# A hybrid encoder layer on one core: first weight units in two pieces, and value rows whose splits are placed later

## The chip, the core and the metric

The kernel runs on one core of a Trainium2 chip. A core has a matrix engine (TensorE, PE in the rows; PEld is its load of stationary weights), a vector engine (VectorE, DVE), a scalar engine (ScalarE, ACT), GpSimd (POOL) and SyncE (SP), which only starts transfers here. Each engine works through its own instructions in the order in which they were written, and waits for the others by semaphores. A transfer runs on up to 16 DMA engines. The metric is the device time of one execution in microseconds.

## The reference, cut to what matters

One encoder layer on a sequence of 512 tokens of width 1024, in float32.

```python
proj = h @ w_in[l]
qa, ka, va, qb, kb, vb = jnp.split(proj, SPLITS, axis=-1)
qa = rope_partial(qa.reshape(b, s, A_Q_HEADS, HEAD_DIM), pos)      # first quarter of each head is rotated
ka = rope_partial(ka.reshape(b, s, A_KV_HEADS, HEAD_DIM), pos)
...
o_a = windowed_gqa_sink(qa, ka, va, a_sink[l]).astype(h.dtype)     # 128-query blocks, window 128, a sink per head
o_b = dilated_mixture(qb, kb, vb).astype(h.dtype)                  # windows (128,1), (512,4), (2048,16)
gates = jax.nn.sigmoid(h @ w_gate[l] + b_gate[l])
g_a, g_b = jnp.split(gates, N_BRANCH, axis=-1)
mixed = g_a * (o_a @ w_br_a[l]) + g_b * (o_b @ w_br_b[l])
y = mixed @ w_out[l]
h = layer_norm(DN_ALPHA * h + y, ln1_g[l], ln1_b[l])
f = (jax.nn.silu(h @ w_ff_gate[l]) * (h @ w_ff_up[l])) @ w_ff_down[l]
h = layer_norm(DN_ALPHA * h + f, ln2_g[l], ln2_b[l])
```

## The kernel before, in words

**Products.** Every operand of a product is split into a high part, rounded to the format that TensorE takes, and the rest (`split`, L349: a copy on ScalarE or VectorE, then a subtraction on VectorE). A product of two operands is three matmuls of 128x512: high by high, high by low, low by high (L453 to L455 in `feat_k`; L626 to L628 for value rows). x stands turned, as eight tiles of 128x512 (`xT`), of which the first four belong to half 0 of a weight unit and the others to half 1. A weight unit has 128 output columns; a half unit is a transfer of 256 KB.

**The order.** No engine's order is written by hand. Each piece of work is an `op` with a cost for each engine that may do it, the tiles that it reads and writes, and a priority. `Program.run` (L170) plays the program through with these costs: at each moment every free engine takes the ready operation of lowest priority number for which buffers are there, and so the instructions are written down. A transfer on SyncE occupies two running counters (start of issue, end of data) and is taken to be done 0.9 us after its data. If a planned transfer is faster than the real one, the operations that need it stand too early in their engine's queue, and all behind them wait as well.

**The start** (`half_unit_by`, L366). The first three half units (a key unit k and two query units q and r of the first mixer) come in three pieces each of 128, 128 and 256 columns (`CUTS`). The table `FIRST` gives the priority of each piece and of each tile of x. PE takes x's tiles one after the other, with nine matmuls each (three units by three). Behind them come a third query unit (q2) and the values.

**Value rows** (`token_values`, L596). For the four residues of a token's place modulo 4 the value rows of both mixers are computed (a row is 24 matmuls: eight weights by three), evicted and written to a scratch tensor in DRAM (`aside`, L638; `va` in the rows). When all four are there, twelve transfers read them back: four for the left 256 columns in blocks of the first mixer (L644), eight of half the size for the right 256 columns in windows of the second (L650). `value_split` (L581) makes high and low parts of 128x256 of each of the eight results: a copy (L332 or L334) and a subtraction (L588).

**Rotation** (`Turn`, L471). The rows to be rotated are gathered into one tile (L482), rotated with cos and sin on VectorE (L493 to L499) and put back (L503). The tables for it, the masks, the sinks and the identity are loaded near the start (L432 to L437).

**Attention** (`unit_a`, L708). For a block of 128 queries and four heads: scores on PE (L575, L576), mask and minimum on VectorE (L724), exponential on ScalarE (L728), sum's reciprocal (L731), normalising (L664 on ScalarE, L666 on VectorE), transposes of the probabilities on PE (L676), their split, and the product with the values (L741, L742). The table `ORDER` lists the stages: `q2 VA T G A0 q3 ...` means query unit 2, value rows, rotation, a gate unit, the four blocks of head group 0 of the first mixer, query unit 3. The dense units (`q`, `k1`, `G`) are the work that PE has beside the attention.

Of the kernel before, what the change touches and what calls it, by code (L numbers as in the profile page):

```python
# [15 lines left out]
P = 128  # L16
S = 512
# [42 lines left out]

CUTS = ((0, 128), (128, 256), (256, 512))
FIRST = {("k", 0): (-1000, -998.2, -997.2), ("q", 0): (-998.8, -998.1, -997.1), ("r", 0): (-998.7, -998, -997),
         ("k", 1): (-996.9,), ("q", 1): (-996.7,), ("r", 1): (-996.6,),
         "x": (-999.9, -998.5, -997.5, -996.95, -996.8, -996.5, -996.4, -996.3)}
N_WS, N_WHL, N_ATT, N_WHL1, N_TWO = 6, 16, 16, 40, 4
# [8 lines left out]
ORDER = """  # L74
q2 VA T G A0 q3 q4 G k1 T A1 q5 G q6 q7 T A2 G G A3 Q00 K00 T V Q02 K02 T Q01 K01 T B0 B1 G g Q10 K10 T g Q12 K12 T Q11 K11 T B2 B3 g8
"""
# [20 lines left out]
class Program:  # L97
# [72 lines left out]
    def run(self):  # L170
# [28 lines left out]
        while n_left:  # L199
# [11 lines left out]
            while progress:  # L211
                progress = False
                for e in engines:
# [65 lines left out]
def dve(n, fast=False, extra=0.0):  # L279
    return 0.069 + (0.00074 if fast else 0.00104) * n + extra  # L280
# [7 lines left out]
def hybrid_layer(ctx: ExitStack, tc: tile.TileContext, wpack, xT, xtok, sink, bgate,  # L288
# [145 lines left out]
    load(mA, maska, abs_prio=-119.3, dst=lambda: mA.t[:, :384])  # L434
    load(nsink, sink.partition_broadcast(P), 0.1, abs_prio=-119.2)
    load(ident, identd, 0.2, abs_prio=-119.1)
    load(bg, bgate, 0.1, abs_prio=-119)  # L437
# [27 lines left out]

    EV, NOW = -100.0, -300.0

# [3 lines left out]
    class Turn:  # L471
# [16 lines left out]
        def turn(self):  # L488
# [3 lines left out]
            toks = [(t, i, hh) for i in range(n) for hh in range(2)]  # L492
            op([(DVE, dve(S, extra=0.03))], lambda e: nc.vector.stream_shuffle(w.t[r], t.t[r], SHUF), reads=toks,  # L493
               writes=[w], prio=EV)
# [85 lines left out]

    def value_split(ps, c0, toks):  # L581
# [4 lines left out]
        op(cp_alts(256, True), lambda e: copy(e, v()[:, :, 0:64], src()), reads=toks,  # L586
           writes=[(t, "h"), (t, "room")], prio=EV)
        op([(DVE, dve(256))], lambda e: nc.vector.tensor_tensor(  # L588
            v()[:, :, 64:128], src(), f32(v()[:, :, 0:64]), op=ALU.subtract),
           reads=[*toks, (t, "h")], writes=[(t, "l")], prio=EV)  # L590
        return t
# [4 lines left out]
    def token_values(dilated):  # L596
# [43 lines left out]
        if not dilated:  # L640
            raw = [slot() for _ in range(NR)]
            every = [(aside, r) for r in range(NR)]
            for m, t in enumerate(raw):
                op([(SP, 0.37)], lambda e, t=t, m=m: nc.sync.dma_start(  # L644
                    t.t[:, 0:256], aside.t[:, 32 * m:32 * m + 32, 0:256]), reads=every, writes=[(t, 0)], prio=EV)
# [950 lines left out]
```

## Time and profile before

| | |
|---|---|
| median of 3 runs | 792.73 us (792.34 to 793.79) |
| profiled execution | 792.01 us, of which the span is 790.2 us |
| TensorE busy | 770.3 us, 97% of the span |
| VectorE, ScalarE busy | 651.1 us (82%), 482.6 us (61%) |
| transfers | 113.36 MB, mean 143 GB/s |
| granted clock of TensorE | 0.991 over the span |
| chain that ended last | PE 89%, DMA 5%, SPq 3%, ACT 2%, DVE 1% |

A row of the timeline gives start, duration, engine, source line, operation and tiles; a bracket behind it tells how long the engine stood idle just before and what ended that. SPq is SyncE issuing a transfer. Durations of pipelined matmuls overlap, so their distance from start to start is their real cost. A helper has one line for all who call it: L332 is every copy by ScalarE, L334 every copy by VectorE.

### The profile page before, as it was taken

To read this page: it belongs to the slowest core of one execution; us is meant where nothing else is said; L and a number is where in the kernel's file an instruction comes from. 1 tells how busy PE (TensorE), PEld (TensorE's weight loads), DVE (VectorE), ACT (ScalarE), POOL (GpSimd) and SP (SyncE) were. 2 spreads that over 40 slices of the span, in tenths; PEclk is the share of its full clock that TensorE was granted. 3 is DMA by queue.
4 is the path that set the end of the run, shared out by engine and by line. 5 is a ranking of instruction groups with operands and counts; after the bars stand their busy time and mean duration, and the time that the engine had idled before them with its cause. 6 is when DMAs were issued, how large, how long until landed. Compare 5 with 4: busy or idle time off the path is not lost.

```text
span 790.2 us, 13367 instructions
## 1 busy us (share of the span) xinstructions
PE 770.3 (97%) x4470; PEld 677.4 (86%) x4470; DVE 651.1 (82%) x1370; ACT 482.6 (61%) x1066; POOL 124.1 (16%) x288
## 2 busy tenths in 40 slices
PE   8996999999999999999999999999999999999996
PEld 5785888888888888888888899999999999999985
DVE  5385887988899999688686999888888889788697
ACT  5455667778687787596252557655655655555631
POOL 0010000001001701600011011134112330123002
PEclk9997999999999999999999999999999999999999
DMA  7744222313132225154465188779876987689202
GB/s 243 216 151 152 84 79 93 100 46 117 38 106 92 82 82 169 55 188 158 139 206 109 50 216 251 174 171 202 221 197 149 227 203 210 168 221 201 66 1 107
DMA packets 69221, 113.36 MB, mean 143 GB/s; under 512 B 8608, under 2 KB 17440, under 8 KB 69152
## 3 DMA queue, kind: packets, MB, share of 16 engines
q1 hardware_dynamic: 57488, 91.47, 35.7%
q0 software_dynamic: 11520, 20.98, 16.3%
q8 instruction: 35, 0.57, 0.3%
q14 instruction: 34, 0.28, 0.1%
q10 hardware_dynamic: 144, 0.07, 0.0%
HBM read 104.87 MB, written 4.72 MB: 139 GB/s over the span
## 4 chain that ended last, share of the span: by engine, by line
PE 89%; DMA 5%; SPq 3%; ACT 2%; DVE 1%; issue 1%; DVEq 0%; ACTq 0%
PE ps L453 10%; PE ps L454 10%; PE ps L455 9%; PE ps L1310 9%; PE ps L1309 9%; PE ps L1308 9%; PE ps L1437 4%; PE ps L1438 4%; PE ps L1439 4%; PE ps L676 3%; PE ps L1075 3%; PE ps L1074 3%; PE ps L1073 3%; PE ps L576 1%; PE ps L575 1%; PE ps L742 1%
## 5 line engine op out<-in xcount | busy, mean ns | idle before, releaser
L332 ACT ACTIVATE sl<-sl 128x512 fp32r<-128x512 f32 (+4 forms) x452 | 243.5, 568 | 82.9 <-PE ps L454 21.3
L1192 DVE TENSOR_TENSOR sl<-sl,sl 128x512 fp32r<-128x512 f32 (+3 forms) x304 | 170.0, 604 | 10.8 <-ACT sl L332 7.5
L332 ACT ACTIVATE sl<-ps 128x256 f32<-128x256 f32 (+4 forms) x202 | 88.1, 455 | 102.0 <-PE ps L1310 66.0
L453 PE MATMUL ps<-x,sl 128*128 128x512 f32 x304 | 121.9, 401 | 1.0 <-ACT x L332 1.0
L454 PE MATMUL ps<-x,sl 128*128 128x512 f32 x304 | 119.8, 394 | 0.3 <-DVE x L429 0.2
L455 PE MATMUL ps<-x,sl 128*128 128x512 f32 x304 | 119.2, 392 | 0.0
L353 DVE TENSOR_TENSOR sl<-sl,sl 128x512 fp32r<-128x512 f32 x114 | 75.4, 686 | 8.7 <-ACT sl L332 7.9
L1262 POOL DMA_DIRECT2D sl<-wpack x44 | 40.7, 982 | 266.3 <-DVE sl L1192 109.4
L1308 PE MATMUL ps<-x,sl 128*128 128x256 f32 x264 | 74.8, 283 | 0.0
L1310 PE MATMUL ps<-x,sl 128*128 128x256 f32 x264 | 74.7, 283 | 0.0
L1309 PE MATMUL ps<-x,sl 128*128 128x256 f32 x264 | 74.7, 283 | 0.0
L1192 DVE TENSOR_TENSOR sl<-sl,ps 128x512 f32<-128x512 f32 (+1 forms) x78 | 47.4, 611 | 25.7 <-PE ps L1310 16.6
L455 PEld LDWEIGHTS ps<-x,sl 128*128 128x128 f32 x304 | 57.4, 189 | 12.7
L453 PEld LDWEIGHTS ps<-x,sl 128*128 128x128 f32 x304 | 57.7, 190 | 11.3 <-ACT x L332 1.5
L454 PEld LDWEIGHTS ps<-x,sl 128*128 128x128 f32 x304 | 57.6, 190 | 10.4 <-DVE x L429 1.2
L1309 PEld LDWEIGHTS ps<-x,sl 128*128 128x128 f32 x264 | 50.6, 192 | 0.5
L1308 PEld LDWEIGHTS ps<-x,sl 128*128 128x128 f32 x264 | 50.6, 192 | 0.5
L1310 PEld LDWEIGHTS ps<-x,sl 128*128 128x128 f32 x264 | 50.6, 192 | 0.0
L1310 PE MATMUL ps<-tw,sl 128*128 128x256 f32 x176 | 49.8, 283 | 0.0
L1309 PE MATMUL ps<-tw,sl 128*128 128x256 f32 x176 | 49.8, 283 | 0.0
L1310 PE MATMUL ps<-sl,sl 128*128 128x256 f32 x176 | 49.8, 283 | 0.0
L1308 PE MATMUL ps<-tw,sl 128*128 128x256 f32 x176 | 49.8, 283 | 0.0
(150 smaller groups left out, 1862.7 us busy)
## 6 DMA issues: line engine op xcount, KB each, us to landing
sl<-wpack SPq DMA_DIRECT2D x235, 256.0 KB
sl<-wpack POOLq DMA_DIRECT2D x44, 256.0 KB, 5.3
wf<-wpack SPq DMA_DIRECT2D x36, 256.0 KB
wf<-wpack POOLq DMA_DIRECT2D x36, 256.0 KB, 6.4
sl<-sl SPq DMA_DIRECT2D x88, 32.0 KB
sl<-wpack SPq DMA_DIRECT2D x19, 128.0 KB
sl<-xT SPq DMA_DIRECT2D x8, 256.0 KB
sl<-xtok SPq DMA_DIRECT2D x8, 256.0 KB
```

The costliest lines, as they stand in the source:

```text
L332: nc.scalar.activation(dst, src, AF.Copy)
L353: op([(DVE, dve(S))], lambda e: nc.vector.tensor_tensor(l.t, src.t, f32(h.t), op=ALU.subtract), reads=[src, h], writes=[l], prio=prio, abs ...
L453: mm(o, a, x0, start=(k == 0), stop=False)
L454: mm(o, a, x1, start=False, stop=False)
L455: mm(o, b, x0, start=False, stop=(k == nk - 1))
L1192: op([(DVE, dve(w))], lambda e: nc.vector.tensor_tensor(dst(), x(), y(), op=o), reads=reads, writes=writes, prio=prio)
L1262: return op([(POOL, 1.0)], lambda e: nc.gpsimd.dma_start(dst.t, wpack[u, :, j * S:(j + 1) * S], accum_op=ALU.add), reads=[dst], writes=[ds ...
L1308: mm(o, wh, bh[k](), start=(first and k == 0), stop=False, skip_group_check=True)
L1309: mm(o, wh, bl[k](), start=False, stop=False, skip_group_check=True)
L1310: mm(o, wl, bh[k](), start=False, stop=(k == 3), skip_group_check=True)
L1437: mm(ps.t, x0, w[0].t, start=(first and m == 0), stop=False, skip_group_check=True)
L1438: mm(ps.t, x0, w[1].t, start=False, stop=False, skip_group_check=True)
```

## The change

It has four parts.

- The first three half units come in two pieces, of 128 and 384 columns. In `FIRST`, x's second tile stands ahead of the second pieces, and x's third and fourth tile right behind them.
- The priorities of the tables (cos, sin, mask, sinks, identity) are raised from about -119 to -95, that is, later.
- The planner takes each read of value rows to be slower: costs of 0.6 and 0.75 instead of 0.37 and 0.18, and 4 us more to landing (`READ`, added to `o.done`). The reads of the right 256 columns and their splits get a priority of +30 instead of -100 (`LATER`).
- In `ORDER`, query unit 3 stands ahead of head group 0. And the shuffle of the rotation now also names the whole tile `t` among what it reads.

```diff
-CUTS = ((0, 128), (128, 256), (256, 512))
-FIRST = {("k", 0): (-1000, -998.2, -997.2), ("q", 0): (-998.8, -998.1, -997.1), ("r", 0): (-998.7, -998, -997),
+CUTS = ((0, 128), (128, 512))
+FIRST = {("k", 0): (-1000, -998.3), ("q", 0): (-999.7, -998.1), ("r", 0): (-999.6, -998),
...
-         "x": (-999.9, -998.5, -997.5, -996.95, -996.8, -996.5, -996.4, -996.3)}
+         "x": (-999.9, -998.4, -997.9, -997.8, -997.4, -997, -996.9, -996.8)}
...
-q2 VA T G A0 q3 q4 G k1 T A1 q5 G q6 q7 T A2 G G A3 Q00 K00 T V ...
+q2 VA T G q3 A0 q4 G k1 T A1 q5 G q6 q7 T A2 G G A3
+Q00 K00 T V ...
...
-                        o.done = dma[1] + 0.9
+                        o.done = dma[1] + 0.9 + o.moves
...
-    for t_, src, ap in ((cosT, ropec, -119.3), (sinT, ropes, -119.2)):
+    for t_, src, ap in ((cosT, ropec, -95.3), (sinT, ropes, -95.2)):
...
-    EV, NOW = -100.0, -300.0
+    EV, NOW, LATER, READ = -100.0, -300.0, 30.0, 4.0
...
-                op([(SP, 0.37)], lambda e, t=t, m=m: nc.sync.dma_start(
-                    t.t[:, 0:256], aside.t[:, 32 * m:32 * m + 32, 0:256]), reads=every, writes=[(t, 0)], prio=EV)
+                op([(SP, 0.6)], lambda e, t=t, m=m: nc.sync.dma_start(
+                    t.t[:, 0:256], aside.t[:, 32 * m:32 * m + 32, 0:256]), reads=every, writes=[(t, 0)], prio=EV, moves=READ)
...
-                    op([(SP, 0.18)], lambda e, t=t, h=h, c=c: nc.sync.dma_start(
+                    op([(SP, 0.75)], lambda e, t=t, h=h, c=c: nc.sync.dma_start(
                         t.t[64 * h:64 * h + 64, 256:512], aside.t[:, c:c + 16, 256:512]), reads=every, writes=[(t, 1, h)],
-                       prio=EV)
+                       prio=LATER, moves=READ)
             for g in range(2):
                 for m, t in enumerate(raw):
-                    res[g].append(value_split(t, 256 * g, [(t, 1, h) for h in range(2)] if g else [(t, 0)]))
+                    res[g].append(value_split(t, 256 * g, [(t, 1, h) for h in range(2)] if g else [(t, 0)],
+                                              LATER if g else EV))
```

The rows below are the engines' instructions in their order, with line, operation and tiles. In the changed kernel the lines are one or two higher. First, SyncE from its first transfer, before (`xT` is a tile of x; `wpack` with 128 or 256 columns is a piece of a first half unit; the first piece of k is issued by ScalarE):

```order
L340 DMA sl_74<-xT 128x512
L377 DMA sl_76<-wpack 128x128
L377 DMA sl_78<-wpack 128x128
L340 DMA sl_80<-xT 128x512
L377 DMA sl_71<-wpack 128x128
L377 DMA sl_76<-wpack 128x128
L377 DMA sl_78<-wpack 128x128
L340 DMA sl_86<-xT 128x512
L377 DMA sl_71<-wpack 128x256
L377 DMA sl_76<-wpack 128x256
L377 DMA sl_78<-wpack 128x256
L340 DMA sl_94<-xT 128x512
```

and the same place now:

```order
L341 DMA sl_74<-xT 128x512
L378 DMA sl_76<-wpack 128x128
L378 DMA sl_78<-wpack 128x128
L341 DMA sl_80<-xT 128x512
L378 DMA sl_71<-wpack 128x384
L378 DMA sl_76<-wpack 128x384
L378 DMA sl_78<-wpack 128x384
L341 DMA sl_86<-xT 128x512
L341 DMA sl_88<-xT 128x512
```

The third tile of x keeps its place, behind three larger pieces; the fourth moves from twelfth to ninth.

Second, SyncE at the end of the value weights (L609, eight in all, each as two transfers, of which the rows show the last five before) and the gathers for the rotation (L482, from evicted rows of k, q and r), before:

```order
L609 DMA sl_235<-wpack 128x2x128 x2
L609 DMA sl_280<-wpack 128x2x128 x2
L609 DMA sl_289<-wpack 128x2x128 x2
L482 DMA sl_298<-sl_286 16x512 x2
L609 DMA sl_303<-wpack 128x2x128 x2
L482 DMA sl_298<-sl_300 16x512 x2
L609 DMA sl_325<-wpack 128x2x128 x2
L482 DMA sl_298<-sl_315 16x512 x2
```

and now:

```order
L610 DMA sl_220<-wpack 128x2x128 x2
L610 DMA sl_268<-wpack 128x2x128 x2
L610 DMA sl_278<-wpack 128x2x128 x2
L610 DMA sl_288<-wpack 128x2x128 x2
L610 DMA sl_298<-wpack 128x2x128 x2
L483 DMA sl_308<-sl_294 16x512 x2
L483 DMA sl_308<-sl_296 16x512 x2
L341 DMA sl_323<-wpack 128x512
L483 DMA sl_308<-sl_313 16x512 x2
```

The seventh and eighth value weight now go out ahead of all gathers.

Third, ScalarE in the first attention block: L332 of 128x4x64 is the split of a gathered value tile (those that read sl_616, sl_618, sl_620, sl_622 here are the right 256 columns), L728 an exponential, L664 a normalising. Before:

```order
L332 ACTIVATE sl_717<-sl_616 128x4x64
L728 ACTIVATE sl_655,st_653<-sl_655,st_653 128x257
L728 ACTIVATE sl_693,st_715<-sl_693,st_715 128x385
L332 ACTIVATE sl_734<-sl_618 128x4x64
L664 ACTIVATE sl_641<-sl_641,st_653 128x256
L332 ACTIVATE sl_743<-sl_620 128x4x64
L664 ACTIVATE sl_647<-sl_647,st_653 128x256
L664 ACTIVATE sl_649<-sl_649,st_653 128x256
L664 ACTIVATE sl_655<-sl_655,st_653 128x256
L332 ACTIVATE sl_760<-sl_622 128x4x64
```

and now:

```order
L730 ACTIVATE sl_675,st_705<-sl_675,st_705 128x257
L333 ACTIVATE sl_719<-sl_582 128x512
L730 ACTIVATE sl_681,st_705<-sl_681,st_705 128x257
L730 ACTIVATE sl_683,st_705<-sl_683,st_705 128x257
L333 ACTIVATE sl_738<-sl_602 128x4x64
L730 ACTIVATE sl_686,st_705<-sl_686,st_705 128x257
L333 ACTIVATE sl_758<-sl_604 128x4x64
L730 ACTIVATE sl_736,st_746<-sl_736,st_746 128x385
L666 ACTIVATE sl_675<-sl_675,st_705 128x256
L666 ACTIVATE sl_683<-sl_683,st_705 128x256
L666 ACTIVATE sl_686<-sl_686,st_705 128x256
```

Two of the four right splits, and one of the four normalisings, now stand on VectorE; the other two splits still stand ahead of the normalisings. On PE, 75 matmuls of 128x512 lie between the last value row and the first transposes, where there were 54.

More of the change, by code (lines that the diff above doesn't have):

```diff
@@ L431, in hybrid_layer @@
     cosT, sinT, mA, mB = slot(), slot(), slot(), slot()
-    for t_, src, ap in ((cosT, ropec, -119.3), (sinT, ropes, -119.2)):
+    for t_, src, ap in ((cosT, ropec, -95.3), (sinT, ropes, -95.2)):
         load(t_, src[0:16].unsqueeze(0).broadcast_to([8, 16, S]), abs_prio=ap)
-    load(mA, maska, abs_prio=-119.3, dst=lambda: mA.t[:, :384])
-    load(nsink, sink.partition_broadcast(P), 0.1, abs_prio=-119.2)
-    load(ident, identd, 0.2, abs_prio=-119.1)
+    load(mA, maska, abs_prio=-95.3, dst=lambda: mA.t[:, :384])
+    load(nsink, sink.partition_broadcast(P), 0.1, abs_prio=-95.2)
+    load(ident, identd, 0.2, abs_prio=-95.1)
     load(bg, bgate, 0.1, abs_prio=-119)
@@ L492, in turn @@
             toks = [(t, i, hh) for i in range(n) for hh in range(2)]
-            op([(DVE, dve(S, extra=0.03))], lambda e: nc.vector.stream_shuffle(w.t[r], t.t[r], SHUF), reads=toks,
+            op([(DVE, dve(S, extra=0.03))], lambda e: nc.vector.stream_shuffle(w.t[r], t.t[r], SHUF), reads=[*toks, t],
                writes=[w], prio=EV)
@@ L578, in scores, with value_split @@
         return go, [(qt, "h"), (qt, "l"), (kt, "h"), (kt, "d"), (kl, "h"), (kl, "d")]
-    def value_split(ps, c0, toks):
+    def value_split(ps, c0, toks, prio=-100.0):
         t = slot(F32R)
```

8 lines of the change are left out of this document (4 added, 4 removed).

## The prediction

> **What bounds the kernel now.** I read the page first: engines, then the chain that ended last.
>
> ```profile
> span 790.2 us, 13367 instructions
> ...
> PE 770.3 (97%) x4470; PEld 677.4 (86%) x4470; DVE 651.1 (82%) x1370; ACT 482.6 (61%) x1066; POOL 124.1 (16%) x288
> ```
>
> TensorE is busy for 97% of the span, so a gain can only come from the time in which its stream of matmuls stops or runs slowly. The change touches the stretch from the start to the end of attention, about 340 us; the question is how much the stream loses there. The timeline of PE shows three stops in the first 82 us; from 80 to 340 us it is never idle (the table further down). The columns are start, duration, engine and line, operation, and in brackets the idle time and what ended it.
>
> ```profile
> 11.12 0.39 PE L455 MATMUL ps<-x,sl 128*128 128x512 f32 x1
> 12.56 0.50 PE L453 MATMUL ps<-x,sl 128*128 128x512 f32 x1 [1.05 <-ACT x L332]
> 13.29 0.50 PE L454 MATMUL ps<-x,sl 128*128 128x512 f32 x1 [0.23 <-DVE x L429]
> 13.63 0.40 PE L455 MATMUL ps<-x,sl 128*128 128x512 f32 x1
> ...
> 33.39 0.39 PE L628 MATMUL ps<-sl,x 128*128 128x512 f32 x1
> 35.25 0.50 PE L626 MATMUL ps<-sl,x 128*128 128x512 f32 x1 [1.48 <-ACT sl L332]
> 35.98 0.50 PE L627 MATMUL ps<-sl,x 128*128 128x512 f32 x1 [0.23 <-DVE sl L614]
> 36.32 0.39 PE L628 MATMUL ps<-sl,x 128*128 128x512 f32 x1
> ...
> 67.14 0.39 PE L454 MATMUL ps<-x,sl 128*128 128x512 f32 x1
> 67.37 0.39 PE L455 MATMUL ps<-x,sl 128*128 128x512 f32 x1
> 73.57 0.48 PE L676 MATMUL ps<-ident,sl 128*128 128x128 f32 x1 [5.81 <-ACT sl L664]
> 75.48 2.13 PE L676 MATMUL ps<-ident,sl 128*128 128x128 f32 x7 [1.43 <-ACT sl L664]
> 77.26 0.78 PE L453 MATMUL ps<-x,sl 128*128 128x512 f32 x1
> ...
> 80.26 0.40 PE L454 MATMUL ps<-x,sl 128*128 128x512 f32 x1
> ```
>
> Two matmuls of 128x512 in a full stream start 0.23 us apart (67.14 and 67.37; durations overlap). So the losses, start to start, are:
> - start-up: 11.12 to 13.63 is 2.51 us for three steps of 0.23, a loss of 1.83 (the fourth tile of x is late);
> - value rows: 33.39 to 36.32 is 2.93 for three steps, a loss of 2.25 (the eighth value weight is late);
> - first attention block: 67.37 to 80.26 is 12.89 us. In it stand eight steps of 0.23 and eight transposes, which the chain of waits shows at 0.87 us for eight when nothing holds them. That is 2.69, so the loss is 10.2.
>
> ```profile
> 83.16 0.87 PE ps L676 x8
> ```
>
> The third loss is part wait, part slow clock. The table by stretches gives PE's busy time, the granted clock (PEclk), the DMA share and GB/s:
>
> ```profile
> 5.00:10.00 5.00, 4.94 (x22) 3.82 (x22) 3.64 (x12) 2.96 (x8) 0.00 (x0) 1.00 0.77 246
> 32.31:35.72 3.41, 1.94 (x8) 1.07 (x6) 0.83 (x2) 0.73 (x2) 0.00 (x0) 1.00 0.50 140
> 66.44:69.84 3.40, 1.32 (x6) 0.75 (x4) 1.79 (x6) 0.97 (x4) 0.00 (x0) 1.00 0.27 94
> 69.86:73.26 3.40, 0.00 (x0) 0.00 (x0) 2.73 (x9) 2.83 (x9) 0.00 (x0) 0.50 0.59 199
> 80.00:340.00 260.00, 260.00 (x1334) 220.90 (x1332) 225.98 (x577) 192.42 (x461) 44.01 (x184) 1.00 0.29 91
> ```
>
> The clock falls to half at about 69.85, little over two microseconds after PE's last matmul, and PE is fully busy again from 80. Half clock costs 2.4 us of the 10.2: seven transposes took 77.26 - 75.48 = 1.78 where 0.76 is full speed, and seven matmuls 80.26 - 77.26 = 3.00 where 1.6 is.
>
> What PE waits for at 67.6 is ScalarE, and ScalarE waits for the gather of value rows:
>
> ```profile
> 65.49 0.42 ACT L332 ACTIVATE sl<-sl 128x256 fp32r<-128x256 f32 x1 [4.33 <-DMA sl<-va]
> ...
> 74.61 0.42 ACT L332 ACTIVATE sl<-sl 128x256 fp32r<-128x256 f32 x1 [1.09 <-DMA sl<-va]
> 74.93 1.29 ACT L664 ACTIVATE sl<-sl,st 128x256 f32<-128x256 f32 x3
> 76.30 0.42 ACT L332 ACTIVATE sl<-sl 128x256 fp32r<-128x256 f32 x1
> ```
>
> Splits of gathered value rows (128x256) stand in ScalarE's queue between the exponentials (L728) and the normalising (L664) that the transposes need. The queue is in order, so the softmax moves at the pace of the twelve gathers.
>
> **The change, part by part.**
>
> *Start-up (cuts, x's tiles).* SyncE's own rows, with those of ScalarE for x:
>
> ```profile
> 5.93 0.43 SPq L340 DMA_DIRECT2D sl<-xT x1
> ...
> 7.88 0.63 ACT L332 ACTIVATE x<-sl 128x512 fp32r<-128x512 f32 x1 [0.59 <-DMA sl<-xT]
> ```
>
> The fourth tile of x, issued at 5.93 as SP's twelfth transfer, becomes its ninth: three issues of 0.43 us fewer stand before it, so it starts 1.3 us earlier with the same bytes ahead of it, and should no longer hold PE. The third tile keeps its place but has 384 KB more ahead of it (three pieces of 192 KB for three of 64): at the 246 GB/s of 5 to 10 us that is 1.6 us, from 7.88 to 9.5; ScalarE's 0.63 later its first matmul can go, and the second, which needs the low part, 0.73 after that (as from 12.56 to 13.29): 10.9, where PE comes to it at about 9.5. So the third tile's matmuls would lose 1.4 and the gain is 0.4. If the larger pieces fill the holes in the DMA (share 0.77), the tile is some 1 us earlier and the gain 1.3. I take 0.8; the ends are -0.5 (first pieces late too) and 1.83 (no loss left). The three splits and subtractions that fall away cost PE nothing: both engines have idle time in 5 to 10 us (2.96 and 3.64 busy of 5).
>
> *Tables later.* They keep their place: on SP they still stand right behind x's last tile and ahead of the first value weights, and only the gates' bias moves by three rows. Price 0.
>
> *Value weights.* This comes out of the same table of numbers. Before, gathers for the rotation (L482), which wait for an eviction, stood between the sixth, seventh and eighth value weights:
>
> ```profile
> 29.43 1.15 SPq L482 DMA_DIRECT2D sl<-sl x2
> 30.61 1.09 SPq L609 DMA_DIRECT2D sl<-wpack x2
> ...
> 61.41 2.33 SPq L644 DMA_DIRECT2D sl<-va x4
> ```
>
> Now all eight weights stand ahead of them. Two pairs of L482 at 1.15 each (and their waits) leave the front of the eighth weight, at least 2.3 us, against a loss of 2.25. I take 2.25, less 0.4 because the gate's first weight, split behind the rotation's copies, is then what PE reaches early. Ends: 1.0 and 2.25.
>
> *Value splits and q3.* PE now has 75 matmuls of 128x512 between the last value row and the first transposes, where it had 54: 21 more, 4.8 us of work, in front of the wait. On ScalarE the order is better by half: two late splits (right pieces, first and second tile) still stand ahead of the normalising, the other two now run on VectorE. Reads start 3.05 earlier by the terms above, at 61.41 - 3.05 = 58.4 (the fourth row's eviction, now VectorE's, stands behind six subtractions: up to 1.5 later). Before, the normalising ended 74.93 + 1.29 - 61.41 = 14.8 us after the first read; in that lay a wait of 1.09 for the third late split and its 0.42, which now stand elsewhere. Without them it is 13.3, with the delay only moved 14.8; and a weight load of 256 KB now stands between the reads, up to 1.1 us at the 246 GB/s above. Between 13.3 and 15.9 I take 14.7, about the middle: the probabilities are ready at 58.4 + 14.7 = 73.1. PE arrives at 67.60 - 3.05 + 0.4 + 4.8 = 69.75 and waits 3.4. Ends: 2.0 (chain of 13.3) and 6.1 (late eviction, chain of 15.9). If the clock falls again it costs the 2.4 of before, and the block after it, whose normalising stands behind twelve ScalarE rows (I allow 1 us of wait at full clock), hides in the slow stretch. So the stage loses 5.8, or 4.4 if the clock holds, instead of 10.2: a gain of 4.4, or 5.8.
>
> *Sum.* 0.8 + 2.25 - 0.4 + 4.4 = 7.05. The profiled execution took 792.01, of which 1.8 lie around the span; it becomes 784.96. It was 0.72 under the median 792.73, so in terms of the median I forecast **785.7**.
>
> **The clock, by row and by rule.** In the stretch 66.44 to 69.84 PE was busy for 1.32 of 3.40 us and the clock still fell at its end; in 32.31 to 35.72 it was busy for 1.94 of 3.41 and the clock held. So a wait of 3.4 is long enough if 2 us of it fall in one such stretch, which I hold likely. The Trainium skill, "TensorE: Matmul & The Clock Gate", section "Part 1: The HAM clock gate", says that the array goes to half rate after at least one idle window of some 3.4 us of a free-running clock. By that rule a wait of 3.4 hardly ever covers a whole window and the clock holds; by the row, a window that is two thirds idle is enough. The measurement decides for me, but a chance is left to the rule.
>
> **Rivals.**
> 1. *The clock holds*: same waits, no half-clock stretch, 5.8 from the stage: 792.73 - 8.45 = 784.3. For it: the wait is half as long as before. Against it: the row 66.44:69.84.
> 2. *The chain of reads slips*: late eviction and a chain of 15.9 us: PE loses 6.1 + 2.4, a gain of 1.7 there, 4.35 in all: 788.4. For it: two late splits still ahead of the normalising, and more evictions (q3, q4) waiting behind. Against it: the reads' queue starts emptier.
> 3. *VectorE takes the gain back*: it is busy for 226 of 260 us between 80 and 340. If PE comes 7 us early with 4.8 us of filler already spent, the attention's last blocks end when VectorE lets them: 792.7. For it: those 87%. Against it: the 34 us left idle are five times the gain.
> 4. *Slower*: the later blocks of the first head group have less filler between their scores and transposes, so PE stops again at the second, third and fourth block's transposes. One such stop costs some 2.5 of wait and 2.4 of half clock, 4.9; from the second on it outweighs 7.05: two give 792.73 + 9.8 - 7.05 = 795.5. For it: q3 and q4 are evicted late on both engines. Against it: in the rows of before PE never waits after 80.26.
>
> **How the numbers follow.** The forecast (clock falls) has 0.42, rival 1 0.23, rival 2 0.18, rival 3 0.09, rival 4 0.08. The likeliest one's own range is 783.5 to 788. For 8 in 10 the range must reach rival 2 with its bounds above and, with the clock held (1.4), a start-up gain of 1.83 (1.0 more) and a wait of 2.0 (1.4 less), some 4 us under the forecast below: 781.5 to 791.0. It leaves out rivals 3 and 4 (0.17). A measurement of this kernel tells a change from none at about 0.2%, 1.6 us: faster 0.83 (the forecast, 1 and 2), same 0.09, slower 0.08.
>
> **What would show it.** Right: PE without a stop over 0.5 us near 33; a single stop before the first transposes, at about 70 and of 2.5 to 4.5 us, ended by a normalising; the first value split on ScalarE at about 62; span near 783. Wrong start-up: PE idle over 1.5 us in total before 15. Wrong value weights: a wait for the eighth weight is still there. Wrong on the third part: a stop over 5 us, or several stops between 80 and 130. Two stops of the last kind, or a VectorE without idle time from 80 to 340, would make the whole forecast wrong.

## The result, and the profile after

The changed kernel takes 784.35 us (median of 4 runs, 783.35 to 786.15) against 792.56 us for the kernel before beside it (792.34 to 793.79): a ratio of 0.9896, 95% interval 0.9875 to 0.9917. The forecast was 785.7 us. The profiled execution took 784.13 us, its span is 782.3 us, 7.9 us less than before.

The total came out close to the forecast, and partly by luck: the start-up and the gate's first weight brought 1.9 us less than I had taken, the first attention block 2.85 us more. The experiments also show that the reason which I gave for the largest term was the wrong one.

The page's engine lines of the changed kernel:

```profile
span 782.3 us, 13384 instructions
...
PE 768.7 (98%) x4470; PEld 675.3 (86%) x4470; DVE 648.1 (83%) x1363; ACT 483.3 (62%) x1067; POOL 126.3 (16%) x288
```

PE's timeline in the changed kernel, at the three places where its stream still stops (lines are one or two higher than before):

```profile
9.64 0.40 PE L456 MATMUL ps<-x,sl 128*128 128x512 f32 x1
10.19 0.51 PE L454 MATMUL ps<-x,sl 128*128 128x512 f32 x1
10.91 0.50 PE L455 MATMUL ps<-x,sl 128*128 128x512 f32 x1 [0.22 <-DVE x L430]
11.25 0.39 PE L456 MATMUL ps<-x,sl 128*128 128x512 f32 x1
...
50.05 0.39 PE L629 MATMUL ps<-sl,x 128*128 128x512 f32 x1
51.36 0.50 PE L454 MATMUL ps<-x,sl 128*128 128x512 f32 x1 [0.92 <-ACT sl L333]
51.70 0.40 PE L455 MATMUL ps<-x,sl 128*128 128x512 f32 x1
52.50 0.50 PE L456 MATMUL ps<-x,sl 128*128 128x512 f32 x1 [0.41 <-DVE sl L354]
52.84 0.40 PE L454 MATMUL ps<-x,sl 128*128 128x512 f32 x1
...
71.85 0.40 PE L456 MATMUL ps<-x,sl 128*128 128x512 f32 x1
74.58 1.56 PE L678 MATMUL ps<-ident,sl 128*128 128x128 f32 x8 [2.34 <-ACT sl L666]
75.90 0.48 PE L454 MATMUL ps<-x,sl 128*128 128x512 f32 x1
```

and the stretches that answer to those shown of before:

```profile
5.00:10.00 5.00, 4.88 (x18) 3.03 (x17) 2.80 (x7) 2.88 (x6) 0.00 (x0) 1.00 0.90 317
30.00:36.00 6.00, 6.00 (x29) 4.95 (x28) 1.47 (x3) 0.94 (x2) 0.00 (x0) 1.00 0.66 198
69.73:73.14 3.41, 2.38 (x10) 1.33 (x9) 3.15 (x13) 3.21 (x12) 0.56 (x3) 1.00 0.50 170
73.14:76.55 3.41, 1.89 (x11) 1.42 (x12) 3.20 (x12) 3.41 (x10) 0.00 (x0) 1.00 0.92 288
80.00:340.00 260.00, 260.00 (x1348) 221.06 (x1347) 227.19 (x582) 202.57 (x487) 45.49 (x184) 1.00 0.30 93
```

Start to start, as in the prediction:

- Start-up: 9.64 to 11.25 is 1.61 for three steps of 0.23, 0.92 lost at x's third tile; with 0.58 at the second tile (6.98 to 8.48 for four steps) the loss is 1.5 instead of 1.83. Gain 0.33.
- Value rows: from 30 to 36 us PE is busy without a gap. Gain 2.25.
- Gate's first weight, new: 50.05 to 52.84 is 2.79 for four steps. Loss 1.87.
- First attention block: 71.85 to 75.90 is 4.05 for one step and eight transposes of 0.87 together. The loss is 2.95 instead of 10.2, and the clock holds in both stretches. Gain 7.25.

0.33 + 2.25 - 1.87 + 7.25 = 7.96, which is the difference of the spans. Behind 80 us PE has no wait over 0.1 us; the kernel before has one, of 0.57 us at 343.32.

ScalarE's rows show where the two larger stops come from, and SyncE's when the reads go out:

```profile
44.18 1.28 ACT L333 ACTIVATE sl<-sl 64x512 fp32r<-64x512 f32 x2 [9.43 <-DMA sl<-sl]
...
46.11 3.92 ACT L333 ACTIVATE sl<-sl 64x512 fp32r<-64x512 f32 x6
...
50.67 3.24 ACT L333 ACTIVATE sl<-sl 128x512 fp32r<-128x512 f32 x6
...
66.60 0.42 ACT L333 ACTIVATE sl<-sl 128x256 fp32r<-128x256 f32 x1 [5.24 <-DMA sl<-va]
...
69.54 0.42 ACT L333 ACTIVATE sl<-sl 128x256 fp32r<-128x256 f32 x1 [1.06 <-DMA sl<-va]
...
74.04 1.29 ACT L666 ACTIVATE sl<-sl,st 128x256 f32<-128x256 f32 x3
```

```profile
61.10 2.33 SPq L645 DMA_DIRECT2D sl<-va  x4
```

The gate's first weight (first of the six splits at 50.67) stands behind the rotation's copies (64x512), although ScalarE had been idle for 9.43 us before them. And the softmax of the first block still waits for reads: splits (128x256) stand in front of the normalising (L666).

### The profile page after: what moved, and what is told of

Its sections match the earlier page's. It is cut to its first block, busy times and chain, and to the rows that moved or that the text cites. A ratio compares the mean times of both kernels' runs of the same rounds, so it can differ in the third digit from the quotient of the medians.

```text
span 782.3 us, 13384 instructions
## 1 busy us (share of the span) xinstructions
PE 768.7 (98%) x4470; PEld 675.3 (86%) x4470; DVE 648.1 (83%) x1363; ACT 483.3 (62%) x1067; POOL 126.3 (16%) x288
## 4 chain that ended last, share of the span: by engine, by line
PE 89%; DMA 2%; DVE 1%; SPq 1%; issue 0%; ACT 0%; DVEq 0%; ACTq 0%
PE ps L454 10%; PE ps L455 10%; PE ps L456 10%; PE ps L1312 9%; PE ps L1311 9%; PE ps L1310 9%; PE ps L1439 4%; PE ps L1440 4%; PE ps L1441 4%; PE ps L1077 3%; PE ps L1076 3%; PE ps L1075 3%; PE ps L678 3%; PE ps L577 1%; PE ps L576 1%; PE ps L744 1%
## 5 line engine op out<-in xcount | busy, mean ns | idle before, releaser
L455 PEld LDWEIGHTS ps<-x,sl 128*128 128x128 f32 x304 | 57.3, 188 | 10.2 <-DVE x L430 1.2
```

Source lines behind the costliest of these rows:

```text
L455: mm(o, a, x1, start=False, stop=False)
```

## The experiments

All spans below are of profiled executions. The table gives what PE loses by place, start to start (distance of two matmuls less 0.227 us for 512 columns, 0.17 for 384, 0.12 for 256, 0.11 for a transpose, summed). Half clock is in it, and small gaps beside the stops (3.7 for the changed kernel's first block, where the stop itself is 2.95). From 100 to 295 and behind 380 us every kernel loses some 3 to 4 us together, which the table leaves out. Parts of the change are called by number: 1 start, 2 tables, 3 costs and priority of the reads (READ, LATER), 4 query unit 3 in front. "tw" is the first mixer's output, and "places" are the planner's places for parts of weights.

Executions of the kernel before beside these runs took 790.04 to 795.19 us. Part 1 alone, part 4 alone, parts 3 and 4, and the kernel with the tw splits first were run once each. A difference of one or two microseconds between such spans says little; the places in the table carry the argument.

| kernel | span | to 29 | 29-45 | 45-58 | 58-100 | 295-335 | 335-380 |
|---|---|---|---|---|---|---|---|
| before | 790.2 | 2.6 | 2.2 | 0 | 10.4 | 0.4 | 0.9 |
| changed (1 to 4) | 782.3 | 2.3 | 0 | 1.8 | 3.7 | 0.9 | 0 |
| part 1 alone | 795.6 | 2.8 | 0 | 2.9 | 10.7 | 0.4 | 4.2 |
| part 3 alone | 782.7 | 2.2 | 2.2 | 0 | 3.3 | 1.1 | 0 |
| part 4 alone | 805.0 | 3.7 | 2.5 | 0 | 8.7 | 6.8 | 9.1 |
| parts 3 and 4 | 788.5 | 2.0 | 2.5 | 0 | 2.6 | 0.7 | 5.3 |
| changed without 4 | 787.1 | 2.4 | 0 | 3.8 | 1.0 | 0.3 | 5.0 |
| same, tw splits first | 782.1 | 1.8 | 0 | 2.2 | 3.1 | 0.3 | 0 |
| changed, 18 places | 787.4 | 2.4 | 0 | 0 | 8.6 | 0.7 | 2.1 |
| changed, contiguous rows | 778.0 | 1.7 | 0 | 2.0 | 0.2 | 0.4 | 0 |
| before, contiguous rows | 783.9 | 2.1 | 4.3 | 0 | 2.9 | 0.5 | 0.7 |
| changed without 4, 18 places | 784.9 | 2.1 | 0 | 0.2 | 4.3 | 0.6 | 3.8 |
| changed, three edits | 782.5 | 2.1 | 0 | 0.1 | 6.0 | 0.6 | 0.3 |
| same, without 4 | 779.4 | 2.3 | 0 | 0 | 2.9 | 0.6 | 0.3 |

Part 2 has no run: with it and without it the instructions of PE, VectorE, ScalarE and GpSimd stand in the same order row by row, and on SyncE only the gates' bias changes its place. The shuffle that names the whole tile `t` has no run of its own either. The runs that start from the changed kernel have it, those that start from the kernel before do not. It too moves rows in the order of every engine, so what it is worth is open.

### Which part brought the gain

Part 3 alone: `LATER, READ = 30.0, 4.0`, the reads' costs and `prio` of the right halves, nothing else.

> The kernel before with only the planner's costs for the reads of value rows (READ) and the lower priority of the right halves (LATER); query unit 3 stays behind head group 0. Theory 1 (ScalarE's queue): what holds PE at the first block is that splits of rows which have not landed stand ahead of the exponentials. Here none stands ahead of the first block's four exponentials and its normalising; they go from 60.6 us on at some 0.55 each and the probabilities are ready at about 64.6 to 66 us, when PE, with 12 matmuls less in front, comes to the transposes at 64.9. Loss of the first block 0 to 2 us instead of 10.2, no half clock, span about 780 to 782 us. Theory 2 (filler, on which my prediction's term rests): the 21 matmuls of query unit 3 that now stand in front are the gain; without them, and with 12 fewer, PE waits as long as before or longer: loss 10 to 13 us, span 790 to 793 us.

Measured: 784.32 us, ratio 0.9883 (0.9867 to 0.9900): the time of the whole change. ScalarE, then PE:

```profile
60.25 0.50 ACT L729 ACTIVATE sl<-sl,st 128x257 f32<-128x257 f32 x1
...
62.00 0.50 ACT L729 ACTIVATE sl<-sl,st 128x257 f32<-128x257 f32 x1
...
63.02 1.29 ACT L665 ACTIVATE sl<-sl,st 128x256 f32<-128x256 f32 x3
```

```profile
64.58 1.03 PE L677 MATMUL ps<-ident,sl 128*128 128x128 f32 x8
...
69.78 0.50 PE L743 MATMUL ps<-sl,sl 128*128 128x512 f32 x1 [1.19 <-DVE sl L682]
```

The exponentials and the normalising are through by 64.3, no split before them, and the transposes go at 64.58 without a wait. What is left is a stop of 1.19 at the product with the values and small gaps. Theory 1 holds for the stop before the transposes; it had the size a little too small, with 3.3 us lost where it allowed 0 to 2.

Part 4 alone:

```diff
-q2 VA T G A0 q3 q4 G k1 ...
+q2 VA T G q3 A0 q4 G k1 ...
```

> The kernel before with only query unit 3 ahead of head group 0. Theory 2 (filler): PE has 21 more matmuls, 4.8 us, and comes to the first transposes at 72.4 us instead of 67.6; with the probabilities ready at 73.6 to 76 as before it loses 1 to 4 us there and the clock holds: span about 782 to 786 us. Theory 1 (queue): the planner now puts five splits of gathered rows, three of them of the late right halves, ahead of the first exponential; the third of these lands at about 74.5 us by the landing times of before, so the probabilities are ready only at 78 to 81 us, PE waits 6 to 8 us and the clock falls: loss 8 to 11 us, span about 789 to 791 us.

Measured: 806.82 us (one run), 14.8 us of span slower than before. ScalarE and PE at the first block:

```profile
66.51 0.42 ACT L333 ACTIVATE sl<-sl 128x256 fp32r<-128x256 f32 x1 [4.52 <-DMA sl<-va]
...
76.03 0.42 ACT L333 ACTIVATE sl<-sl 128x256 fp32r<-128x256 f32 x1 [2.44 <-DMA sl<-va]
...
81.17 1.29 ACT L665 ACTIVATE sl<-sl,st 128x256 f32<-128x256 f32 x3
```

```profile
71.48 0.39 PE L456 MATMUL ps<-x,sl 128*128 128x512 f32 x1
75.92 0.44 PE L576 MATMUL ps<-sl,sl 128*128 128x384 f32 x1 [4.06 <-DVE st L725]
...
81.72 1.56 PE L677 MATMUL ps<-ident,sl 128*128 128x128 f32 x8 [1.00 <-ACT sl L665]
```

21 matmuls more in front, and the block still loses 8.7 us: later scores let the planner put five splits, of reads that land as late as 76 us, ahead of the first exponential. The loss lies in the 8 to 11 us of theory 1. Theory 2 (filler, that is dense work for PE in front of the wait), on which my prediction rested, falls. Neither theory had the span: 6.8 us are lost near 313 us (PE waits 3.58 us for a copy by ScalarE, which had itself stood 4.40 us for a transfer; the cause of that was not followed) and 9.1 near 360 and 367 us, at the subtractions on tw (below).

Parts 3 and 4 together:

> The kernel before with READ and LATER and with query unit 3 ahead of head group 0, without the new tables of the start. READ and LATER alone made 782.7 us, the order alone 805.0. If what matters is how many splits of gathered rows stand ahead of the softmax on ScalarE (here one to four ahead of the four exponentials and five ahead of the first normalising, with the order alone five and six), this lies between: a stop of 3 to 7 us at the first block, and since the fourth subtraction on tw stands behind a long run of weight subtractions here, a stop of some 3.4 us and half clock near 355 us: span 787 to 793 us. If query unit 3 as filler covers the wait once the costs of the reads are right, the first block has no stop over 1 us, and the span is 781 us or a little more.

Measured: 790.29 us (one run). The first block loses 2.6 in all, less than the 3 to 7 that I expected: with the costs right, filler does cover most of the wait for the splits that stand ahead of the softmax here. The price is paid near 352 us (5.3 us), as expected there.

The changed kernel without part 4:

> The changed kernel with query unit 3 back behind head group 0, everything else as changed. Theory 1 (queue): no split of gathered rows stands ahead of the first block's softmax, so the stop of 2.95 us before the first transposes shrinks to 0 to 1.5 us, and nothing takes its place: span about 779.5 to 781.5 us against 782.3, so this kernel is 1 to 3 us faster than the changed one. Theory 2 (filler): the stop grows by the 4.8 us of matmuls that no longer stand in front, to 7.5 us or more, and the clock falls for 2.4 us more: span about 787 to 790 us.

Measured: 788.89 us, ratio 0.9949 (0.9924 to 0.9974): 4.8 us of span slower than the changed kernel. The stop before the first transposes is gone, as theory 1 has it:

```profile
66.17 1.04 PE L677 MATMUL ps<-ident,sl 128*128 128x128 f32 x8
```

But "nothing takes its place" was wrong: a stop of 3.44 us with half clock stands at 351 us, and the gate's stop costs 3.8 us instead of 1.8, since here the clock fell behind it. So the span lies where theory 2 had put it, for other reasons. The 1.0 us lost at the first block flatters this kernel, since PE comes there late: in the next kernel, with the same order and no half clock at the gate, the transposes go at 64.27, also without a wait, and the block loses 3.1.

### The stop at 351 us

PE and VectorE of the changed kernel without part 4 (tw is the first mixer's output; L353 are subtractions for weights):

```profile
347.19 0.39 PE L453 MATMUL ps<-sl,sl 128*128 128x512 f32 x1
351.01 0.79 PE L454 MATMUL ps<-sl,sl 128*128 128x512 f32 x1 [3.44 <-DVE sl L995]
```

```profile
343.58 0.69 DVE L995 TENSOR_TENSOR sl<-tw,sl 128x512 fp32r<-128x512 f32 x1
...
344.86 5.50 DVE L353 TENSOR_TENSOR sl<-sl,sl 128x512 fp32r<-128x512 f32 x9
350.28 3.09 DVE L995 TENSOR_TENSOR sl<-tw,sl 128x512 fp32r<-128x512 f32 x5
```

PE needs a tile's low part every nine matmuls (2.05 us). Three subtractions on tw stand ahead of nine for weights, the fourth behind. In the changed kernel five stand ahead, and PE does not stop. The edit raises the priority of the splits on tw:

```diff
-    sa = [split_of(..., [(t, b) for b in range(NR)], -20) for t in oa2 for m in range(2)]
+    sa = [split_of(..., [(t, b) for b in range(NR)], -60) for t in oa2 for m in range(2)]
```

> The changed kernel with query unit 3 back behind head group 0 (787.1 us of span), and the splits of the first mixer's outputs (tw) with priority -60 instead of -20, so that the fourth and later subtractions on tw stand ahead of the run of nine weight subtractions on VectorE. If that place is the cause of the stop at 351 us (3.44 us of wait and half clock behind it, 5.0 us together by distances from start to start), the stop is gone and the span is about 782 us; the stop near 51 us stays, with or without 1.65 us of half clock. Rival: VectorE is behind with everything there (it is busy without a gap from 338 to 353 us), and a stop of about the same size appears at the weights' subtractions instead: span 785 to 787 us.

Measured: 783.87 us (one run), span 782.1.

```profile
342.50 3.10 DVE L995 TENSOR_TENSOR sl<-tw,sl 128x512 fp32r<-128x512 f32 x5
```

All eight are done by 345.6, the stop is gone and nothing replaces it. The gate's stop costs 1.6 us less here and the first block 2.1 more, so the 5.0 us at 351 are the whole difference of the spans. An edit at 60 us cost 5.0 us at 350 by moving rows of one queue.

Part 1 alone (the tables CUTS and FIRST):

> The kernel before with only CUTS and FIRST of the change. My account of the changed kernel puts three of its terms down to these two tables: the start-up loses 1.5 us instead of 1.83 (a gain of 0.33, not the 0.8 that I predicted), the wait of 2.25 us for the eighth value weight near 33 us is gone, and a new stop of about 1.9 us stands near 50 us, at the first weight of the gate unit, whose split is late. The first attention block keeps its loss of about 10 us. Span about 790.2 - 0.33 - 2.25 + 1.9 = 789.5 us. Rival: the stop near 50 us comes from the later parts of the change (the planner's costs or the order); then there is none here and the span is about 787.6 us. Second rival: the value weights were brought forward by the tables' priorities; then the stop near 33 us is still there and the span is about 790 us with no stop at 50.

Measured: 797.4 us (one run). The value weights' 2.2 us are gone and the gate's stop is there, so both come from part 1; but the gate's stop is 2.9 us, and 4.2 us are lost near 360 for the same reason as above (five subtractions on tw behind the run). 3.3 of the 5.4 us that part 1 costs by itself lie where none of its rows stand:

```profile
52.91 0.50 PE L453 MATMUL ps<-x,sl 128*128 128x512 f32 x1 [1.91 <-ACT sl L332]
...
360.72 0.50 PE L454 MATMUL ps<-sl,sl 128*128 128x512 f32 x1 [3.43 <-DVE sl L994]
```

### The gate's first weight

The planner has 16 places for high and low parts of weights, and the eight value weights hold them all until the last value row. The edit:

```diff
-N_WS, N_WHL, N_ATT, N_WHL1, N_TWO = 6, 16, 16, 40, 4
+N_WS, N_WHL, N_ATT, N_WHL1, N_TWO = 6, 18, 16, 40, 4
```

> The changed kernel with N_WHL 18 instead of 16 and nothing else. If the planner's places for weight parts are what makes the gate's first weight late, the stop of 1.87 us at 50 to 53 us is gone. But query unit 3 still stands ahead of head group 0 and five value splits ahead of its normalising, so the softmax still waits for the reads from DRAM, which start no earlier: PE comes to the first transposes some 2.5 us earlier (1.87, and three matmuls fewer in front) and waits that much longer, 4.5 to 6 us, and the clock probably falls for 2.4 us. Span about 782 to 786 us: no gain over the changed kernel. Rival (stops add up): the wait at the transposes stays at 2.95 us and the span is about 780.4 us. If the stop at 51 us is still there, the places are not its cause.

Measured: 789.87 us, ratio 0.9976 (0.9961 to 0.9992), slower than the changed kernel, and its span of 787.4 lies over the 782 to 786 that I expected. The stop at 51 us is gone: the places are its cause. But PE then stands at the first block:

```profile
72.30 2.01 PE L678 MATMUL ps<-ident,sl 128*128 128x128 f32 x8 [3.04 <-ACT sl L666]
75.29 0.79 PE L743 MATMUL ps<-sl,sl 128*128 128x512 f32 x1 [0.98 <-ACT sl L333]
```

It loses 8.6 us there with two stretches of half clock, and 2.1 near 355. The gain is moved to the reads and grows there.

The same edit without part 4:

> The changed kernel with query unit 3 back behind head group 0, and 18 instead of 16 places for high and low parts of weights (N_WHL), so that the split of the gate's first weight is placed ahead of the rotation's copies. My theory of three separate stops: the stop at 51.7 us of the kernel without N_WHL (2.07 us, and 1.65 us of half clock behind it) goes, the first attention block stays without a stop (no value split ahead of its softmax), and the stop at 351 us, where in that kernel the fourth subtraction of L995 on tw stood behind nine of L353, comes one subtraction later: the fifth is now behind them, which PE needs 9 matmuls or 2.05 us later, so about 1.4 us in place of 3.44 and no half clock. Span about 787.1 - 2.07 - 1.65 - 3.4 = 780 us, ratio to the kernel before about 0.985. Rival (the gain at the gate is only moved): with the gate's weight early, PE comes to the first block 2 us earlier and waits there for the fourth value row's chain, 2 to 4 us: span 782 to 785 us.

Measured: 786.10 us, ratio 0.9922 (0.9906 to 0.9938), span 784.9. The gate's stop is gone, the first block loses 4.3 instead of 1.0 (the rival, nearly), and near 351 us 1.81 us of wait bring half clock again, 3.8 together where I had counted 1.4. I had taken a short wait to be safe for the clock; it is not (last section). In the three kernels with query unit 3 behind head group 0, the gate and the first block together lose 4.8 us (changed without 4), 5.3 (tw splits first) and 4.5 (18 places), whether the gate's stop is there or not.

### The reads themselves

The reads take four separate runs of the scratch tensor, one for each residue. Here the scratch is two tensors in which each read is one contiguous run of rows:

```diff
-aside = ... dram.tile([NR, P, S], F32, ...)
+left = ... dram.tile([NR, NR, 32, 256], F32, ...)
+right = ... dram.tile([8, NR, 16, 256], F32, ...)
...
-    t.t[:, 0:256], aside.t[:, 32 * m:32 * m + 32, 0:256]
+    t.t[:, 0:256], left.t[m].rearrange("r i c -> (r i) c")
...
-    t.t[64 * h:64 * h + 64, 256:512], aside.t[:, c:c + 16, 256:512]
+    t.t[64 * h:64 * h + 64, 256:512], right.t[c].rearrange("r i c -> (r i) c")
```

> The changed kernel with the scratch rows in two tensors, laid out so that each of the twelve reads takes one contiguous run of rows (128x256 or 64x256) in place of four separate runs; the row writes come in two halves each. Theory (reads): the stop of 2.95 us before the first transposes is the pace of the reads, which in the traces so far land 1.43 us apart for 128 KB and 0.72 us for 64 KB, with a DMA share of 0.27. Spread over all engines they should land at least twice as fast; the last two value splits no longer hold ScalarE, the probabilities are ready 2 to 4 us earlier, and the stop shrinks to under 1 us: span 779.5 to 781 us. Rival (queue): the pace is that of ScalarE's own rows and of the first landing, about 5.5 us after the fourth row's write, which stays; the stop stays at 2 to 3.5 us and the span at 782 to 783 us.

Measured: 779.82 us (779.62 to 780.62), ratio 0.9843 (0.9828 to 0.9859): faster than both kernels, by 4 to 4.5 us than the changed one; its span of 778.0 is below the 779.5 to 781 expected. In the changed kernel, and then here, while the reads run (DMA share and GB/s are the last two columns):

```profile
66.50:70.00 3.50, 3.50 (x20) 3.06 (x19) 1.27 (x5) 1.29 (x4) 0.00 (x0) 1.00 0.31 105
```

```profile
63.00:66.50 3.50, 3.50 (x20) 2.98 (x20) 2.81 (x10) 2.36 (x7) 0.43 (x3) 1.00 0.65 207
```

ScalarE and PE in the kernel with contiguous rows:

```profile
63.24 1.56 ACT L333 ACTIVATE sl<-sl 128x256 fp32r<-128x256 f32 x4 [2.90 <-DMA sl<-va]
...
68.77 1.31 ACT L668 ACTIVATE sl<-sl,st 128x256 f32<-128x256 f32 x3
```

```profile
70.03 0.39 PE L456 MATMUL ps<-x,sl 128*128 128x512 f32 x1
70.26 1.03 PE L680 MATMUL ps<-ident,sl 128*128 128x128 f32 x8
```

The first value split on ScalarE runs 2.3 us after the first read goes out (60.95), where it was 5.5 us (66.60 after 61.10). Three value splits, with a weight's copy between them in the merged row, run without a pause where they stood about 1.47 us apart (66.60 to 69.54 for two steps). The probabilities are ready at 70.1, and PE passes to the transposes with no gap. The theory of the reads holds. The DMA share of 0.31 is about five of 16 engines, and the 0.27 of the kernel before from 66.44 to 69.84, where hardly anything but these reads ran, is 4.3. The Trainium skill, "DMA: Bandwidth & Descriptors", section "Why a DMA increments its semaphore by 16 and not by 1", says that a transfer is spread over the largest number of engines up to 16 that divides the slowest dimension on both sides: four for these reads, 16 for contiguous rows. The trace agrees (0.27 and 0.31 against 0.65, 94 and 105 against 207 GB/s).

The same two tensors in the kernel before, with no part of the change:

> The kernel before with nothing but the two scratch tensors of contiguous rows; no part of the change is in it. If the pace of the reads is the root of the first attention block's 10.2 us, then here, where splits still stand ahead of the softmax and no query unit 3 is in front, the splits hold ScalarE for about 2 us instead of 9: the last split that stands ahead of the normalising is ready at about 66 to 67 us, the probabilities at 68.5 to 70, PE comes at 67.6, waits 1 to 2.5 us and the clock holds; the waits of 1.83 at the start and 2.25 near 33 us stay. Span 781 to 783 us, ratio 0.988 to 0.991: about what the whole change brought. Rival: the order on ScalarE is the root and the reads' pace only a part; the stop is 4 to 6 us, the clock falls, span 785 to 788 us.

Measured: 786.02 us, ratio 0.9929 (0.9909 to 0.9948). The first block loses 2.9 instead of 10.4 us with the clock at full speed, which is the whole of the change's main gain by another way. The span is 0.9 us over what I expected, and 2.1 us more than before are lost at 35 us, where the old wait for the eighth value weight brought half clock this time.

All three edits on the changed kernel, and the same without part 4:

> The changed kernel with all three stops addressed: contiguous scratch rows, 18 places for weight parts, and splits on tw with priority -60. From the kernel with contiguous rows alone (span 778.0 us, ratio 0.9843): the stop of 2.0 us at the gate's first weight goes; PE then comes to the first transposes at about 67.6 us instead of 70.3, the reads start 0.8 us earlier and one split fewer stands ahead, so the probabilities are ready at about 68.9 and 1.3 us of the gain are lost again there; no stop near 350 us. Span about 777.3 us, ratio about 0.983. Rival: the whole 2.0 us come back as a wait at the first transposes, or the clock falls for 1.7 us behind it: span 778 to 780 us.

> The same three edits with query unit 3 back behind head group 0, so that no value split stands ahead of the first softmax. The kernel with 18 places and that order had a span of 784.9 us; of it 3.7 us were the stop near 351 us with its half clock, which the priority -60 takes away, and about 2 of the 4 us that PE loses between 63 and 77 us are waits behind value splits at the reads' pace, which the contiguous rows take away. Span about 779 us. Rival: the 4 us between 63 and 77 us are the softmax's own chain, too short of filler with query unit 3 behind, and stay: span 781 us. In both cases it is not faster than the same kernel with query unit 3 in front.

Measured: 784.15 us, ratio 0.9902 (0.9887 to 0.9917), and 781.02 us, ratio 0.9863 (0.9847 to 0.9880). Neither beats the contiguous rows alone. The first:

```profile
69.85 1.88 PE L680 MATMUL ps<-ident,sl 128*128 128x128 f32 x8 [0.78 <-ACT sl L668]
72.85 0.50 PE L745 MATMUL ps<-sl,sl 128*128 128x512 f32 x1 [1.12 <-ACT sl L333]
```

It has no stop at the gate and none at 350, but its reads go out at 61.74 instead of 60.95, and PE, early by the gate's two microseconds, loses 6.0 us at the first block, 1.7 of them to half clock: more than its rival's 2.0. Its span of 782.5 lies over the 777.3 expected and over its rival's 778 to 780. The second has the expected span (779.4, loss at the first block 2.9), and is faster than the first, against the expectation: with no split ahead of its softmax, that softmax does not wait for the reads. Why the planner's new order makes them later in the first was not tried, nor were contiguous rows with part 3 alone.

## Why the prediction was right and wrong

**Start-up: 0.8 taken, 0.33 measured.** The working was right to 0.1 us (matmuls of x's third tile at 10.1 and 10.9 by the text, 10.19 and 10.91 in the trace); it gave 0.4. The step that failed was to go up to 0.8 in case larger pieces fill the holes in the DMA. They do (share 0.77 to 0.90), yet the third tile came no earlier than the working at 246 GB/s had it; why is not shown. And the working put nothing for x's second tile, where 0.58 us are lost now.

**Tables: 0.** No row but the gates' bias moves.

**Value weights: 2.25.** Measured 2.25. Part 1 alone shows that it belongs to the table FIRST.

**The gate's first weight: 0.4 taken, 1.87 measured.** The step "less 0.4 because the gate's first weight, split behind the rotation's copies, is then what PE reaches early" asked how late the split is by its neighbours and not why it stands there. The cause, shown by 18 places, is the planner's 16 places, which the value weights hold.

**The first attention block: gain 4.4 taken, 7.25 measured.** The wait was sized well: 3.4 by the text, 2.95 measured; the chain from the first read to the probabilities took 75.33 - 61.10 = 14.2 where I took 14.7. Both ends were 2.3 to 2.7 us later than I had them (reads at 61.10, not 58.4; PE at 72.1, not 69.75), so the difference held. The fourth row's eviction waited until 55.38 behind six subtractions, which I had allowed 1.5 us. The mis-sized term is the clock: I gave its fall 0.42 against 0.23 and it held, because the wait lay across two stretches with 2.38 and 1.89 us of work in each. So rival 1 is what happened at this block. That its 784.3 is the measured 784.35 is luck, since it has the start-up and the gate as the forecast has them. Of the signs, the span and the stop before the first transposes came about as written; the first value split on ScalarE came at 66.60, not at about 62, and the stop at the gate was not foreseen.

**The reason for it was wrong.** I credited the gain to query unit 3 as 4.8 us of work in front. Part 4 alone gains 1.7 us in that block, with the clock down again, and costs 14.8 us over the span; part 3 alone brings all that the change brings. And without part 4 the changed kernel has no stop before the first transposes. What counts is what stands on ScalarE ahead of the softmax, and how fast the reads land. I had noted that on ScalarE "the order is better by half" and gave it 1.5 us of the chain. Once part 3 is there, filler covers the wait for the splits that part 4 brings ahead of the softmax, but the block gains little or nothing by it (parts 3 and 4: 2.6 us lost, part 3 alone: 3.3). The 4.8 us that part 4 is worth within the changed kernel come from the gate (3.8 to 1.8) and from near 351 us (5.0 to 0), where none of its rows stand, while the block itself loses 2.7 more.

**Rivals 3 and 4** did not come about in the changed kernel. Rival 3's place (VectorE at the end of attention) is real: six of the other kernels lose 2 to 9 us between 335 and 380 us. In the one that was tested it was not for lack of VectorE time but for the place of rows in its queue.

## What to carry to other kernels

When a planner orders several queues, take a change apart before you believe its parts: here, each taken alone, one part brought everything, one cost at least what it gained, and one lost 14.8 us, nearly all of it 250 to 300 us behind the place that was edited. When an in-order engine waits for transfers, ask first why the transfers are slow: a scratch layout with contiguous reads took the stop away in the changed kernel, which became the best one (ratio 0.9843), and left 2.9 of 10.4 us in the kernel before. Taking away a stop that lies ahead of another wait mostly moved it here: without the gate's stop the first block lost 8.6 instead of 3.7 us, or 4.3 instead of 1.0.

## What the runs showed of the hardware that I had not expected

Short waits can cost half clock. Each fall in the records, but for the one at the program's end, lasts a multiple of 3.41 us, and what precedes it is a stretch of 3.41 us in which PE was at most about half busy. In the changed kernel without part 4 the clock rises at 56.88 and falls again at 350.42, 293.55 us or 86 such stretches later, so the stretches of this trace lie on one grid. The changed kernel without part 4, at the gate's stop, then the kernel before with contiguous rows, at the value rows:

```profile
50.05:53.46 3.41, 1.77 (x8) 0.83 (x7) 3.26 (x6) 3.36 (x7) 1.32 (x3) 1.00 0.44 150
53.46:56.87 3.41, 3.41 (x10) 2.63 (x9) 3.41 (x6) 2.14 (x5) 0.00 (x0) 0.50 0.96 246
```

```profile
32.89:36.30 3.41, 1.56 (x4) 0.77 (x5) 0.69 (x1) 0.63 (x1) 0.00 (x0) 1.00 0.60 193
36.30:39.71 3.41, 3.41 (x9) 2.63 (x8) 0.00 (x0) 0.60 (x1) 0.00 (x0) 0.50 0.94 333
```

The clock fell after stretches with up to 1.77 us of work. It held after 1.89 (the changed kernel at 73.14) and 1.94 (before at 32.31), but also after 1.76 (part 4 alone, from 70.11) and 1.57 (part 1 alone, from 355.72). So the bound lies near half, and busy time in these records does not give it closer. The clock rises again only after a stretch at half clock that is nearly full: not after 2.50 us (part 1 alone, from 75.82) and 2.70 (part 4 alone, from 312.45), but after 2.83 (the changed kernel without part 4, from 350.42). The clock held at the stop near 35 us in the kernel before and fell here. So a stop of 2 us costs 2 or 3.7 us by where it falls in these stretches, and a wait of 2.95 us in two of them cost nothing more. The Trainium skill, "TensorE: Matmul & The Clock Gate", section "Part 1: The HAM clock gate", speaks of an idle window of some 3.4 us that runs free. The length and the free running agree with the records. A window need only be about half idle by these rows, and the measurement decides.
